# Row-wise first load and nearer stores in a bias-and-softmax kernel

## The chip, the core and the metric

The kernel runs on one core of a Trainium2 chip. The metric is the device time of one launch in microseconds; the time before is the median of ten runs.

## The reference

The kernel adds a clipped relative position bias to a batch of attention logits and takes a softmax over the last axis. There are 2 x 8 matrices of 2112 x 2112 floats; each of the 8 heads has 33 bias values.

```python
rel_clipped = np.clip(pos[:, None] - pos[None, :], -16, 16) + 16
logits = logits + rel_bias[:, rel_clipped][None]
logits = logits - logits.max(axis=-1, keepdims=True)
exp = np.exp(logits)
return (exp / exp.sum(axis=-1, keepdims=True)).astype(np.float32)
```

285.5 MB come in and 285.5 MB go out. (The kernel leaves out the subtraction of the maximum, which doesn't change the quotient.)

## The kernel before

The 33,792 rows are dealt out to the 128 partitions, 264 consecutive rows to each. A chunk is R = 4 rows of every partition: 128 x 8448 floats, 4224 KB, and there are N = 66 chunks. Five buffers L0 to L4 hold chunks; a chunk is loaded, changed in place and stored from the same buffer.

Four queues work on them, each with its order written out by hand, and they meet through semaphores:

- SP (`block.sync`) loads the first five chunks, one DMA each, then for each later chunk waits until the store from its buffer has landed (`reload`, L93) and loads again. Its DMAs are queue q1 of the profile.
- DVE (`block.vector`) first builds the strip F (`strip_of`, L140), 2343 floats on each partition, from which the bias of any row is a window. For that it waits for the bias table rbP (the wait ahead of L168). Then, for each chunk (`vec`, L122): wait until it is loaded, two adds of two rows each (L110), and, as soon as the sums of two rows are there, a reciprocal (L129) and two multiplies (L133).
- ACT (`block.scalar`) issues the two DMAs of the bias table (L205), then for each chunk takes the exponentials row by row with the sum beside it (`exps`, L112, L119). ACT also issues the stores (L91), on queue q10. A store is put into `exps` as `first`: it is issued once the first add of that chunk is done, which by DVE's order means that the chunk before has been multiplied to its end.
- POOL fills two small index tables at the start.

Before the change the store of chunk n - 2 is issued in the exponentials of chunk n ("two chunks behind"), from chunk 2 on; chunk 65, the last, issues stores 63 and 64, and store 65 follows when DVE has finished. The loops take five chunks a turn so that each body names a fixed buffer; what is left over is written out.

A wait takes the semaphore down again by what it waited for (`take`, L84), so that the same constants serve in every turn. L85 in the profile is that wait.

Of the kernel before, what the change touches and what calls it, by code (L numbers as in the profile page):

```python
# [14 lines left out]
def kernel(  # L15
# [14 lines left out]

    nc = tc.nc
    P = 128
    B, H, S, S2 = logits.shape
# [4 lines left out]
    T = S // Q  # L40
    assert Q * B * H == P and T * Q == S and T % W == 0
    M = T // W
    R = 4
    HALF = 2
    BUFS = 5
    N = T // R
# [2 lines left out]
    NB = (FW - 2 * MR) // W  # L49
    assert NB * W + 2 * MR == FW  # L50
    RS = R * S
    PASSES = (N - BUFS - 1) // BUFS
    REST = PASSES * BUFS

    const = ctx.enter_context(tc.tile_pool(name="const", bufs=1))
    F = const.tile([P, FW], FP32, tag="F", name="F")
# [8 lines left out]
    L = [const.tile([P, RS], FP32, tag=f"L{u}", name=f"L{u}") for u in range(BUFS)]  # L65
    tot = [const.tile([P, R], FP32, tag=f"tot{u}", name=f"tot{u}") for u in range(BUFS)]

    def rows(t, start):
        return bass.AP(
            tensor=t.tensor, offset=t.offset + start * S, ap=[[T * S, P], [1, RS]]  # L70
        )

    section = ctx.enter_context(tc.tile_critical(name="rows"))  # L73
    loaded = [nc.alloc_semaphore(f"loaded{u}") for u in range(BUFS)]
# [9 lines left out]
    def take(eng, sem, v):  # L84
        eng.wait_ge(sem, v).then_inc(sem, -v)  # L85

    def load(eng, u, start):
        eng.dma_start(out=L[u][:], in_=rows(logits, start)).then_inc(loaded[u], 16)

    def store(eng, u, start):  # L90
        eng.dma_start(out=rows(out, start), in_=L[u][:]).then_inc(stored[u], 16)  # L91

    def reload(eng, u, start):  # L93
        take(eng, stored[u], 16)
        load(eng, u, start)

    def add(eng, u, s0, start):
        x = L[u]
        x3 = bass.AP(
            tensor=x.tensor,  # L100
            offset=x.offset + (s0 + HALF - 1) * S,
            ap=[[list(x.ap[0])[0], P], [-S, HALF], [1, S]],
        )

        F3 = bass.AP(
            tensor=F.tensor,
            offset=(F.offset + T - HALF - s0) - start,
            ap=[[list(F.ap[0])[0], P], [1, HALF], [1, S]],
        )
        eng.tensor_tensor(out=x3, in0=x3, in1=F3, op=ALU.add).then_inc(added, 1)  # L110

    def exps(eng, u, first):  # L112
        for s0 in range(0, R, HALF):
            take(eng, added, 1)
            if s0 == 0:
                first()
            for i in range(s0, s0 + HALF):
                x = L[u][:, i * S : (i + 1) * S]
                e = eng.activation(out=x, in_=x, func=EXP, accum_out=tot[u][:, i : i + 1])  # L119
            e.then_inc(summed, 1)  # L120

    def vec(eng, u, start, last=False):  # L122
        take(eng, loaded[u], 16)
        for s0 in range(0, R, HALF):
            add(eng, u, s0, start)
        for s0 in range(0, R, HALF):
            take(eng, summed, 1)
            t = tot[u][:, s0 : s0 + HALF]
            eng.reciprocal(out=t, in_=t).then_inc(inverted, 1)  # L129
            take(eng, inverted, 1)  # L130
            for i in range(s0, s0 + HALF):
                x = L[u][:, i * S : (i + 1) * S]
                e = eng.tensor_scalar_mul(out=x, in0=x, scalar1=tot[u][:, i : i + 1])  # L133
        if last:
            e.then_inc(scaled, 1)

    def strip_of(eng):  # L140

        assert M * Q & (M * Q - 1) == 0
        low = rbP[:, W - 1 : W]
        high = rbP[:, 0:1]
        pitch = list(F.ap[0])[0]
        blocks = bass.AP(tensor=F.tensor, offset=F.offset + MR, ap=[[pitch, P], [W, NB], [1, W]])
        rev = bass.AP(
            tensor=rbP.tensor,
            offset=rbP.offset + W - 1,
            ap=[[list(rbP.ap[0])[0], P], [0, NB], [-1, W]],  # L150
        )

        def wide(t):
            return bass.AP(
                tensor=t.tensor, offset=t.offset, ap=[[list(t.ap[0])[0], P], [1, NB], [0, W]]
            )

        def step(ins):
            ins.then_inc(strip, 1)
            take(eng, strip, 1)  # L160

        take(eng, blocks_ready, 2)
        step(eng.tensor_single_scalar(out=qi[:], in_=qi[:], scalar=M * Q - 1, op=ALU.bitwise_and))  # L163
        step(eng.tensor_tensor(out=qm[:], in0=qi[:], in1=mm[:], op=ALU.subtract))  # L164
        for m, op in ((eq, ALU.is_equal), (lt, ALU.is_gt), (gt, ALU.is_lt)):
            step(eng.tensor_scalar(out=m[:], in0=qm[:], scalar1=0.0, scalar2=None, op0=op))  # L166
        take(eng, table, 16 * B)
        step(eng.tensor_scalar(out=rest[:], in0=lt[:], scalar1=low, scalar2=None, op0=ALU.mult))  # L168
        step(eng.tensor_copy(out=F[:, 0:MR], in_=low.to_broadcast([P, MR])))  # L169
        step(  # L170
            eng.scalar_tensor_tensor(  # L171
                out=rest[:], in0=gt[:], scalar=high, in1=rest[:], op0=ALU.mult, op1=ALU.add
            )
        )
        step(eng.tensor_copy(out=F[:, FW - MR : FW], in_=high.to_broadcast([P, MR])))  # L175
        step(eng.tensor_tensor(out=blocks, in0=wide(eq), in1=rev, op=ALU.mult))  # L176
        step(eng.tensor_tensor(out=blocks, in0=blocks, in1=wide(rest), op=ALU.add))  # L177

    with nc.Block() as block:  # L179

        @block.sync
        def _(eng):
            for u in range(BUFS):
                load(eng, u, u * R)
            with eng.Fori(BUFS * R, (REST + BUFS) * R, BUFS * R) as i:
                for u in range(BUFS):
                    reload(eng, u, i + u * R)
            for n in range(REST + BUFS, N):
                reload(eng, n % BUFS, n * R)
            for n in range(N - BUFS, N):  # L190
                take(eng, stored[n % BUFS], 16)

        @block.gpsimd
        def _(eng):
            eng.iota(qi[:], pattern=[[0, NB]], base=0, channel_multiplier=M).then_inc(  # L195
                blocks_ready, 1
            )
            eng.iota(mm[:], pattern=[[1, NB]], base=1 - M, channel_multiplier=0).then_inc(  # L198
                blocks_ready, 1
            )  # L200

        @block.scalar
        def _(eng):
            for b in range(B):
                eng.dma_start(  # L205
                    out=rbP[b * H * Q : (b + 1) * H * Q],
                    in_=bass.AP(
                        tensor=rel_bias.tensor,
                        offset=rel_bias.offset,
                        ap=[[W, H], [0, Q], [1, W]],  # L210
                    ),
                ).then_inc(table, 16)
            def none():
                pass

            def behind(u, start):
                return lambda: store(eng, (u - 2) % BUFS, start - 2 * R)

            for n in range(2):
                exps(eng, n, none)  # L220
            with eng.Fori(2 * R, (REST + 2) * R, BUFS * R) as i:
                for u in range(BUFS):
                    exps(eng, (u + 2) % BUFS, behind(u + 2, i + u * R))
            for n in range(REST + 2, N - 1):
                exps(eng, n % BUFS, behind(n, n * R))
            exps(
                eng,
                (N - 1) % BUFS,
                lambda: [store(eng, n % BUFS, n * R) for n in (N - 3, N - 2)],
            )  # L230
            take(eng, scaled, 1)
            store(eng, (N - 1) % BUFS, (N - 1) * R)

        @block.vector
        def _(eng):
            strip_of(eng)
            with eng.Fori(0, REST * R, BUFS * R) as i:
                for u in range(BUFS):
                    vec(eng, u, i + u * R)
            for n in range(REST, N):  # L240
                vec(eng, n % BUFS, n * R, last=n == N - 1)


# [28 lines left out]
```

## Time and profile before

| what | us |
|---|---|
| median of ten runs | 1353.92 (1351.43 to 1354.94) |
| the profiled execution's own time | 1355.21 |
| its span | 1353.4 |
| DVE busy | 960.6 |
| ACT busy | 527.0 |
| bytes moved | 571.00 MB, 422 GB/s over the span |

The span is the time that the profiler covers; what lies around it, 1.8 us, is start and end of the launch. Busy times of the engines overlap each other. The row "DMA" of the page divides the span into 40 slices of 33.8 us and gives the busy share of the 16 DMA engines in each, in tenths.

### The profile page before, as it was taken

The numbers are of one execution on the slowest core, as the hardware profiler recorded it, in microseconds if no ns is written. First come the engines' busy times: TensorE is split into PE (matmuls) and PEld (weight loads), VectorE is DVE, ScalarE is ACT, GpSimd is POOL, SyncE is SP. The second block draws the span as 40 slices with busy tenths as digits, with TensorE's granted clock in tenths as the row PEclk, the third lists the DMA queues.
The fourth block names the chain that finished last, engine by engine and source line by source line (L and its number), as shares of the span: only waits on it lengthen the run. The fifth ranks groups of instructions, "written<-read, shape, count | busy, mean of one in ns | idle before, by whom it ended". The sixth has DMA issues, their size and how long they took to land. (4 is left out here: it accounts for less than half of the span.)

```text
span 1353.4 us, 2458 instructions
## 1 busy us (share of the span) xinstructions
DVE 960.6 (71%) x539; ACT 527.0 (39%) x529; POOL 0.5 (0%) x6
## 2 busy tenths in 40 slices
DVE  1888776776776677677677677677667767767762
ACT  0544433442442443443343344244244334334432
POOL 0000000000000000000000000000000000000000
DMA  9579999999999999999999999999999999999988
GB/s 395 245 318 430 432 431 432 431 433 438 433 433 431 432 431 432 431 433 438 435 431 431 431 433 430 432 438 435 433 431 431 431 432 431 433 439 434 432 376 384
DMA packets 19155, 571.00 MB, mean 422 GB/s; under 512 B 2256, under 2 KB 2256, under 8 KB 2256
## 3 DMA queue, kind: packets, MB, share of 16 engines
q1 hardware_dynamic: 9504, 285.48, 49.1%
q10 hardware_dynamic: 9648, 285.50, 48.9%
q14 instruction: 3, 0.02, 0.0%
HBM read 285.49 MB, written 285.47 MB: 422 GB/s over the span
## 5 line engine op out<-in xcount | busy, mean ns | idle before, releaser
L119 ACT ACTIVATE L<-L 128x2112 f32<-128x2112 f32 x264 | 516.0, 1955 | 761.9 <-ACTq L85 761.6
L110 DVE TENSOR_TENSOR L<-L,F 128x4224 f32<-128x4224 f32 x132 | 595.7, 4554 | 230.3 <-DVEq L85 230.3
L133 DVE TENSOR_SCALAR L<-L,tot 128x2112 f32<-128x2112 f32 x264 | 336.3, 1316 | 20.1 <-DVEq L85 0.5
L129 DVE RECIPROCAL tot<-tot 128x2 f32<-128x2 f32 x132 | 21.9, 166 | 93.3 <-DVEq L85 93.3
L119 ACT ACTIVATION_READ_ACCUMULATOR L<-L 128x1 f32 x264 | 49.2, 186 | 0.0
L168 DVE TENSOR_SCALAR rest<-lt,rbP 128x71 f32<-128x71 f32 x1 | 0.3, 257 | 24.4 <-DVEq L85 24.4
L119 ACT ACT_TABLE_LOAD x1 | 1.3, 1283 | 39.6 <-ACTq L85 39.6
L176 DVE TENSOR_TENSOR F<-eq,rbP 128x2343 f32<-128x2343 f32 x1 | 2.6, 2600 | 0.1
L177 DVE TENSOR_TENSOR F<-F,rest 128x2343 f32<-128x2343 f32 x1 | 2.6, 2599 | 0.1
L163 DVE TENSOR_SCALAR qi<-qi 128x71 int32<-128x71 int32 x1 | 0.2, 198 | 1.5 <-DVEq L85 1.5
L171 DVE SCALAR_TENSOR_TENSOR rest<-gt,rbP,rest 128x71 f32<-128x71 f32 x1 | 0.3, 293 | 0.2 <-DVEq L85 0.2
L164 DVE TENSOR_TENSOR qm<-qi,mm 128x71 f32<-128x71 int32 x1 | 0.2, 233 | 0.1
L166 DVE TENSOR_SCALAR eq<-qm 128x71 f32<-128x71 f32 x1 | 0.2, 198 | 0.2 <-DVEq L85 0.2
L166 DVE TENSOR_SCALAR lt<-qm 128x71 f32<-128x71 f32 x1 | 0.2, 197 | 0.1
L166 DVE TENSOR_SCALAR gt<-qm 128x71 f32<-128x71 f32 x1 | 0.2, 197 | 0.1
L169 DVE COPY F<-rbP 128x16 f32<-128x16 f32 x1 | 0.2, 175 | 0.1
L175 DVE COPY F<-rbP 128x16 f32<-128x16 f32 x1 | 0.2, 175 | 0.1
L195 POOL IOTA qi<- 128x71 int32 x1 | 0.2, 187 | 0.6 <-SPq L73 0.6
L198 POOL IOTA mm<- 128x71 int32 x1 | 0.2, 187 | 0.0
L256 POOL MEMSET const-bfloat16-1.0<- 128x1 bf16 x1 | 0.1, 101 | 0.0
L256 POOL MEMSET const-uint8-127<- 128x1 uint8 x1 | 0.1, 101 | 0.0
L256 POOL MEMSET const-float32-0.0<- 128x1 f32 x1 | 0.1, 98 | 0.2 <-issue 0.2
(1 smaller groups left out, 0.1 us busy)
## 6 DMA issues: line engine op xcount, KB each, us to landing
L<-in_logits_dram SPq DMA_DIRECT2D x66, 4224.0 KB, 27.3
out_dram<-L ACTq DMA_DIRECT2D x66, 4224.0 KB, 27.4
rbP<-in_rel_bias_dram ACTq DMA_DIRECT2D x2, 8.2 KB
```

The costliest lines, as they stand in the source:

```text
L110: eng.tensor_tensor(out=x3, in0=x3, in1=F3, op=ALU.add).then_inc(added, 1)
L119: e = eng.activation(out=x, in_=x, func=EXP, accum_out=tot[u][:, i : i + 1])
L129: eng.reciprocal(out=t, in_=t).then_inc(inverted, 1)
L133: e = eng.tensor_scalar_mul(out=x, in0=x, scalar1=tot[u][:, i : i + 1])
L163: step(eng.tensor_single_scalar(out=qi[:], in_=qi[:], scalar=M * Q - 1, op=ALU.bitwise_and))
L164: step(eng.tensor_tensor(out=qm[:], in0=qi[:], in1=mm[:], op=ALU.subtract))
L166: step(eng.tensor_scalar(out=m[:], in0=qm[:], scalar1=0.0, scalar2=None, op0=op))
L168: step(eng.tensor_scalar(out=rest[:], in0=lt[:], scalar1=low, scalar2=None, op0=ALU.mult))
L171: eng.scalar_tensor_tensor(out=rest[:], in0=gt[:], scalar=high, in1=rest[:], op0=ALU.mult, op1=ALU.add)
L176: step(eng.tensor_tensor(out=blocks, in0=wide(eq), in1=rev, op=ALU.mult))
L177: step(eng.tensor_tensor(out=blocks, in0=blocks, in1=wide(rest), op=ALU.add))
L256: nc = _bacc.Bacc("TRN2", target_bir_lowering=False, num_devices=1)
```

## The change

- The first chunk is loaded with four DMAs, one for each row of a partition, on the same semaphore; DVE waits once until all four have landed and sets the counter back to what its ordinary wait expects.
- The exponentials of chunks 1 to 5 issue the store of the chunk before (one behind). Those of chunk 6 issue none. From chunk 7 on the store is two behind, as before. Chunk 64 issues stores 62 and 63, chunk 65 store 64, and store 65 follows at the end.
- The three loops are made by one helper, `passes`, which takes the range of chunks; the places where the loops start and end move a little.

```diff
-    def rows(t, start):
+    def rows(t, start, run=RS):
         return bass.AP(
-            tensor=t.tensor, offset=t.offset + start * S, ap=[[T * S, P], [1, RS]]
+            tensor=t.tensor, offset=t.offset + start * S, ap=[[T * S, P], [1, run]]
         )
...
+    def passes(eng, n0, n1, body):
+
+        k = (n1 - n0) // BUFS * BUFS
+        with eng.Fori(n0 * R, (n0 + k - BUFS) * R + 1, BUFS * R) as i:
+            for u in range(BUFS):
+                body((n0 + u) % BUFS, i + u * R)
+        for n in range(n0 + k, n1):
+            body(n % BUFS, n * R)
...
         @block.sync
         def _(eng):
-            for u in range(BUFS):
+            for r in range(R):
+                eng.dma_start(
+                    out=L[0][:, r * S : (r + 1) * S], in_=rows(logits, r, S)
+                ).then_inc(loaded[0], 16)
+            for u in range(1, BUFS):
                 load(eng, u, u * R)
-            with eng.Fori(BUFS * R, (REST + BUFS) * R, BUFS * R) as i:
-                for u in range(BUFS):
-                    reload(eng, u, i + u * R)
-            for n in range(REST + BUFS, N):
-                reload(eng, n % BUFS, n * R)
+            passes(eng, BUFS, N, lambda u, start: reload(eng, u, start))
...
         @block.scalar
...
-            for n in range(2):
-                exps(eng, n, none)
-            with eng.Fori(2 * R, (REST + 2) * R, BUFS * R) as i:
-                for u in range(BUFS):
-                    exps(eng, (u + 2) % BUFS, behind(u + 2, i + u * R))
-            for n in range(REST + 2, N - 1):
-                exps(eng, n % BUFS, behind(n, n * R))
-            exps(
+            def out_of(*ns):
+                return lambda: [store(eng, n % BUFS, n * R) for n in ns]
+
+            exps(eng, 0, out_of())
+            for n in range(1, NEAR - 1):
+                exps(eng, n % BUFS, out_of(n - 1))
+            exps(eng, (NEAR - 1) % BUFS, out_of())
+            passes(
                 eng,
-                (N - 1) % BUFS,
-                lambda: [store(eng, n % BUFS, n * R) for n in (N - 3, N - 2)],
-            )
+                NEAR,
+                N - 2,
+                lambda u, start: exps(
+                    eng, u, lambda: store(eng, (u - 2) % BUFS, start - 2 * R)
+                ),
+            )
+            exps(eng, (N - 2) % BUFS, out_of(N - 4, N - 3))
+            exps(eng, (N - 1) % BUFS, out_of(N - 2))
             take(eng, scaled, 1)
             store(eng, (N - 1) % BUFS, (N - 1) * R)
...
         @block.vector
         def _(eng):
             strip_of(eng)
-            with eng.Fori(0, REST * R, BUFS * R) as i:
-                for u in range(BUFS):
-                    vec(eng, u, i + u * R)
-            for n in range(REST, N):
-                vec(eng, n % BUFS, n * R, last=n == N - 1)
+            eng.wait_ge(loaded[0], 16 * R).then_inc(loaded[0], 16 - 16 * R)
+            passes(eng, 0, N - 1, lambda u, start: vec(eng, u, start))
+            vec(eng, (N - 1) % BUFS, (N - 1) * R, last=True)
```

NEAR is 7.

More of the change, by code (lines that the diff above doesn't have):

```diff
@@ L51 @@
     RS = R * S
-    PASSES = (N - BUFS - 1) // BUFS
-    REST = PASSES * BUFS
+    NEAR = 7
     const = ctx.enter_context(tc.tile_pool(name="const", bufs=1))
@@ L212, in _ @@
                 ).then_inc(table, 16)
[L213 to L217, printed above, removed]
-            for n in range(2):
-                exps(eng, n, none)
-            with eng.Fori(2 * R, (REST + 2) * R, BUFS * R) as i:
-                for u in range(BUFS):
-                    exps(eng, (u + 2) % BUFS, behind(u + 2, i + u * R))
-            for n in range(REST + 2, N - 1):
-                exps(eng, n % BUFS, behind(n, n * R))
-            exps(
-                eng,
-                (N - 1) % BUFS,
-                lambda: [store(eng, n % BUFS, n * R) for n in (N - 3, N - 2)],
-            )
+            def out_of(*ns):
[5 more added lines that the diff above has]
+            passes(
+                eng,
+                NEAR,
[3 more added lines that the diff above has]
+                ),
+            )
+            exps(eng, (N - 2) % BUFS, out_of(N - 4, N - 3))
+            exps(eng, (N - 1) % BUFS, out_of(N - 2))
             take(eng, scaled, 1)
```

## The prediction

> **What bounds the kernel now.** I read the page's first three parts, then the chain, then the busy time by stretches of the span, then the timeline at both ends.
>
> ```profile
> span 1353.4 us, 2458 instructions
> DVE 960.6 (71%) x539; ACT 527.0 (39%) x529; POOL 0.5 (0%) x6
> DMA  9579999999999999999999999999999999999988
> q1 hardware_dynamic: 9504, 285.48, 49.1%
> q10 hardware_dynamic: 9648, 285.50, 48.9%
> HBM read 285.49 MB, written 285.47 MB: 422 GB/s over the span
> ```
>
> No engine is full; the 16 DMA engines are, except in slices 2, 3 and the last two. The load queue (q1) and the store queue (q10) carry the same bytes. The chain of waits is only 2.6 us long (a DVE multiply and a queue step at 1329 to 1331.5): it loses the trail at the stores, so I leave it aside and go by stretches. Columns: stretch, its length, busy time of three engines, clock, DMA share, GB/s.
>
> ```profile
> 0.00:14.00 14.00, 1.02 (x5) 0.00 (x0) 0.52 (x6) 1.00 0.86 348
> 14.00:25.00 11.00, 0.00 (x0) 0.00 (x0) 0.00 (x0) 1.00 1.02 428
> 25.00:35.00 10.00, 6.17 (x7) 0.00 (x0) 0.00 (x0) 1.00 1.01 433
> 35.00:55.00 20.00, 17.58 (x9) 9.18 (x9) 0.00 (x0) 1.00 0.90 387
> 55.00:74.40 19.40, 17.60 (x10) 9.37 (x9) 0.00 (x0) 1.00 0.07 28
> 74.40:95.00 20.60, 18.41 (x12) 12.48 (x15) 0.00 (x0) 1.00 0.93 367
> 95.00:125.00 30.00, 27.06 (x14) 13.79 (x14) 0.00 (x0) 1.00 1.00 424
> ...
> 155.00:1290.00 1135.00, 821.28 (x456) 454.16 (x456) 0.00 (x0) 1.00 1.00 433
> ...
> 1315.00:1332.00 17.00, 14.45 (x8) 7.89 (x8) 0.00 (x0) 1.00 0.75 319
> 1332.00:1353.40 21.40, 0.00 (x0) 0.00 (x0) 0.00 (x0) 1.00 0.84 363
> ```
>
> With loads alone (25 to 35) and with both queues (155 to 1290) the rate is 433 GB/s at share 1.00. 571.00 MB at 433 is 1318.7 us; the other 34.7 us of the span are DMA time not used. By stretch it is length x (1 - rate/433): the start 2.7; 14 to 35 0.1; 35 to 125 2.1 + 18.1 + 3.1 + 0.6 = 24.0; the last two 4.5 and 3.5. These add up to 34.9. So the time is set by the moments in which neither queue has work, and by nothing else. The timeline says why they are empty:
>
> ```profile
> 27.51 0.26 DVE L168 TENSOR_SCALAR rest<-lt,rbP 128x71 f32<-128x71 f32 x1 [24.37 <-DVEq L85]
> 31.75 2.60 DVE L177 TENSOR_TENSOR F<-F,rest 128x2343 f32<-128x2343 f32 x1
> 34.93 9.03 DVE L110 TENSOR_TENSOR L<-L,F 128x4224 f32<-128x4224 f32 x2 [0.58 <-DVEq L85]
> 56.39 1.96 ACT L119 ACTIVATE L<-L 128x2112 f32<-128x2112 f32 x1 [7.60 <-ACTq L85]
> 72.61 0.38 ACTq L91 DMA_DIRECT2D out_dram<-L  x1
> 1319.74 0.82 ACTq L91 DMA_DIRECT2D out_dram<-L  x2
> 1331.62 0.34 ACTq L91 DMA_DIRECT2D out_dram<-L  x1
> ```
>
> DVE waits 24.37 us for the 16 KB bias table; the strip F is done at 34.35, and chunk 0's add starts at 34.93. All five buffers are loaded by about 55; the first store is issued at 72.61, with the exponentials of chunk 2. Between, nothing can move. At the end, stores 63 and 64 are issued at 1319.74, while by the packet records store 62 ends at 1316.4 and the next packets start at 1321.6: a hole of 5.2 us, most of the 4.5 of that stretch.
>
> **The change, part by part.**
> *Row loads beside the bias table.* Chunk 0 comes as four DMAs of 1056 KB, 8,448 bytes a partition, instead of one of 33,792. The packet records show that the bias DMAs use 8 of the 16 engines, 18 small packets on each, and that from 7.3 us on each of these waits for one whole load packet of 1.251 us: 18 x 1.25 = 22, so 27.5 at DVE is explained. A quarter-size packet is 1.251/4 = 0.31 us; with the small packet and the gaps 0.33. 18 x 0.33 = 6, so the table lands near 13.4 us, if its first packet still comes at 7.3. From that point L168 to chunk 0's add is 34.93 - 27.51 = 7.4 us: add at 20.8. Chunk 0 itself has landed by then (14.0 before).
> [...] The packet records show turns of one descriptor: one bias packet every 1.25 us beside 33,792-byte ones. [...]
> Cost of the split: SP issues 8 DMAs instead of 5, at 0.333 us each (the median of the load issues), so its last first-round load leaves at 4.6 instead of 3.6 us; load 1 isn't needed in the queue before 14, and load 5's reload is queued behind them but waits for store 0 anyway. [...] I take 0.7, between 0 and 6.
> DVE's added wait on the four rows (then the counter set back) is one more step in its queue, some 0.1 us (steps of the strip follow each other at 0.1 to 0.2); behind it is only chunk 0's add, which it can't delay beyond the landing.
>
> *Stores one chunk behind at first.* Store 0 moves from the exponentials of chunk 2 to those of chunk 1: 56.39 - 34.93 = 21.5 us after chunk 0's add, so at 20.8 + 21.5 = 42.3 instead of 72.61. Its packets follow 1.8 us later (72.61 to 74.4 before): 44.1, while loads 3 and 4 still run (to 55 alone, to about 65 with the store beside them). So store 0 ends at about 64, load 5 is queued at 66, while store 1 (issued 16 us after store 0, at 58.4) moves. From there one queue always has work: DVE's period of 16.07 us (51.72 to 67.79) is shorter than DMA's 20.0 for a load and a store. So all of the 24.0 goes. ACT's issue of 0.34 us ahead of chunk 1 costs nothing: DVE's period was 16.07 without a store (chunk 1) and with one (chunk 2). If it were uncovered, 5 x 0.34 = 1.7. What is late next: DVE, which in chunks 1 to 7 comes after its loads; DMA doesn't wait for it.
>
> *The switch at chunk 6.* No store is issued there; store 5 goes with chunk 7. Chunk 7's add is at 20.8 + 16.8 + 6 x 16.07 = 134, store 5 in the queue at 141. Store 4 ends, with stores at 20 us each after store 0's 64, at about 144. So the queue has some 3 us left; and if it ran dry, load packets would have the engines to themselves. Cost 0, at most some 5. The middle is as before, two behind: 0 per chunk.
>
> *The last four.* Chunk 64's exponentials issue stores 62 and 63, so 63 is there when 62 ends: -4.5 (the stretch) to -5.2 (the hole). Two issues take 0.82 instead of 0.34 us on ACT, ahead of chunk 64's exponentials; DVE is idle 3.85 us ahead of each late add, which hides it. Store 64 goes at chunk 65's add as before, store 65 after the last multiply, 16.5 us after that add; store 63 and 64 are 20 us of cover. The last stretch's 3.5 us (landing of the last store) stay.
>
> *Loops.* DVE's loop makes 13 turns instead of 12, ACT's body starts elsewhere, register steps of 0.03 to 0.05 us: under DMA, 0.
>
> Sum: -24.0 - 4.5 + 0.7, and 0.5 for seams that remain: -27.3. On the profiled execution's span 1353.4 this gives 1326.1, on its own time 1355.2 it gives 1327.9. The median of the runs is 1.3 below that execution, 1353.9: I predict 1326.6. A floor: 1318.7 + 2.7 + 3.5 = 1324.9 of span.
>
> **The rivals.**
> [...] Chance 0.11.
> *A hole at the switch or at the end*, some 5 us, because the phase between the queues differs: 1331. For it: the slack of about 3 us. Against: both queues must be dry at once. Chance 0.08.
> *Slower: a lower rate in the middle.* Loads and stores then meet at other places of HBM, store boundaries about 3 us from where they were against the loads. If reads and writes disturbed each other there, each per cent of 433 GB/s in the 1135 us would cost 11.4; at 2.4%, below 423 GB/s, all the gain is gone, and at 3% the time is 1361. For it: nothing in the trace excludes it. Against: the rate is the same 433 with loads alone as with both, at share 1.00, so the engines are the limit, not where the data lie. Chance 0.04. That the change does nothing, both holes staying, can't be: store 0's issue doesn't need chunk 2. I leave 0.02 for it and the like.
>
> **How the numbers follow.** The main case, 0.75, lies between the floor, 1324.9 + 0.5, and 1329 (most of the 6 us rule for the DMAs excluded by the rows). The range goes from 1324.5 to 1335, with the second case and most of the first. About 0.2% (2.7 us) is what a measurement of this kernel tells from no change. Faster 0.94, within 0.02, slower 0.04.
>
> **What would show it.** Right: L168 at 13 to 14 us and the first add near 21; first store issued near 42; share 1.00 between 35 and 125; no stretch under 400 GB/s between 1270 and the last landing; 433 in the middle. Wrong in the first step: L168 later than 24, the add later than 32, an empty stretch after 55. Wrong in the switch: a dip at 135 to 160. Wrong in the whole: a middle below 430 GB/s.

## The result and the profile after

The changed kernel takes 1331.34 us (median of nine runs, 1329.72 to 1340.27) against 1354.06 before (30 runs, 1351.43 to 1355.11): ratio 0.9847, 95% interval 0.9834 to 0.9859, so 22.7 us less by the medians. The profiled execution took 1327.64 us, with a span of 1325.9; it is the shortest of the eleven executions on record here. Both numbers matter: the sum of the prediction met the span of that one execution (1326.1 against 1325.9), but the median lies 4.7 us above the predicted 1326.6, inside the range. The page after:

```profile
span 1325.9 us, 2476 instructions
DVE 960.4 (72%) x539; ACT 527.1 (40%) x529; POOL 0.5 (0%) x6
DMA  9999999999999999999999999999999999999998
q1 hardware_dynamic: 9936, 285.48, 50.0%
q10 hardware_dynamic: 9648, 285.50, 49.9%
HBM read 285.49 MB, written 285.47 MB: 431 GB/s over the span
```

The two slices that showed 5 and 7 tenths are full, and the engines' busy times are as they were. q1 has 432 packets more: 3 x 128 data packets of 8,448 bytes, and 3 x 16 of 4 bytes, 16 at the end of each DMA. The same stretches as before the change (stretch, length, busy time of DVE, ACT, POOL, clock, DMA share, GB/s):

```profile
0.00:14.00 14.00, 3.13 (x10) 0.00 (x0) 0.53 (x6) 1.00 0.88 340
...
35.00:55.00 20.00, 17.89 (x10) 8.01 (x8) 0.00 (x0) 1.00 0.98 411
55.00:74.40 19.40, 17.70 (x10) 9.20 (x9) 0.00 (x0) 1.00 1.03 442
74.40:95.00 20.60, 18.57 (x12) 12.44 (x13) 0.00 (x0) 1.00 0.98 422
...
125.00:155.00 30.00, 24.31 (x16) 12.12 (x14) 0.00 (x0) 1.00 1.00 433
155.00:1240.00 1085.00, 787.13 (x437) 435.99 (x437) 0.00 (x0) 1.00 1.00 433
...
1305.00:1325.90 20.90, 0.00 (x0) 0.00 (x0) 0.00 (x0) 1.00 0.80 346
```

The stretch from 55 to 74.4 went from 28 to 442 GB/s. By length x (1 - rate/433), 35 to 95 now loses 1.0 - 0.4 + 0.5 = 1.1 us, where it lost 23.3. The middle stays at 433, and nothing dips at 125 to 155, where the stores go from one chunk behind to two. The timeline at both ends:

```profile
11.29 0.26 DVE L178 TENSOR_SCALAR rest<-lt,rbP 128x71 f32<-128x71 f32 x1 [8.16 <-DVEq L86]
18.83 9.03 DVE L111 TENSOR_TENSOR L<-L,F 128x4224 f32<-128x4224 f32 x2 [0.70 <-DVEq L86]
40.28 0.36 ACTq L92 DMA_DIRECT2D out_dram<-L  x1
...
1273.64 0.94 ACTq L92 DMA_DIRECT2D out_dram<-L  x2
1293.35 0.34 ACTq L92 DMA_DIRECT2D out_dram<-L  x1
1304.96 0.34 ACTq L92 DMA_DIRECT2D out_dram<-L  x1
```

The table is used at 11.29 instead of 27.51, chunk 0's add starts 16.1 us earlier, the first store 32.3 us earlier. The last store goes out at 1304.96, 21 us before the end: nearly two stores of 10 us each (4224 KB at 433 GB/s) are then left to drain.

### The profile page after: what moved, and what is told of

Its sections match the earlier page's. It is cut to its first block, busy times and chain, and to the rows that moved or that the text cites. A ratio compares the mean times of both kernels' runs of the same rounds, so it can differ in the third digit from the quotient of the medians.

```text
span 1325.9 us, 2476 instructions
## 1 busy us (share of the span) xinstructions
DVE 960.4 (72%) x539; ACT 527.1 (40%) x529; POOL 0.5 (0%) x6
## 6 DMA issues: line engine op xcount, KB each, us to landing
out_dram<-L ACTq DMA_DIRECT2D x66, 4224.0 KB, 27.5
```

## The experiments

Each run was timed in rounds beside the kernel before; the three batches had 1353.23, 1353.06 and 1353.32 us for it. Unless said otherwise, the edit is against the changed kernel.

**The changed kernel again**, unedited, in two batches.

> The changed kernel once more, unedited, to see how far its executions lie apart. Its profiled execution had a span of 1325.9 us, 0.2 from the sum, but the median of its runs was 1331.3 and two were at 1338 and 1340. Theory (bytes at 433 GB/s plus the moments without work): 1326 to 1328 of span in every execution, and the later ones are chance. Rival 1 (thin slack of the two-behind middle, about 3 us in each queue, runs dry in some executions): a spread of some 10 us again, while the kernel with one-behind stores throughout shows none. Rival 2 (the start differs between executions): the spread goes with the row loads.

> The changed kernel once more, for the spread (3 of 15 executions so far lay at 1338 to 1340). Thin-slack theory: one or more of five at 1335 to 1340. Median 1330 to 1333 by both.

Medians 1332.62 (1327.53 to 1338.58) and 1330.12 (1327.24 to 1338.62). Of all 22 executions, four lie at 1338 to 1340, the others at 1327 to 1334. The first expectation's theory, a span of 1326 to 1328 in every execution, has fallen. This time the profiled execution was a long one, with a span of 1336.8:

```profile
155.00:900.00 745.00, 538.45 (x298) 296.50 (x297) 0.00 (x0) 1.00 1.00 433
900.00:1300.00 400.00, 282.15 (x159) 157.57 (x160) 0.00 (x0) 1.00 1.00 428
1300.00:1336.80 36.80, 14.46 (x8) 8.01 (x8) 0.00 (x0) 1.00 0.74 318
```

The first profile of the same kernel over the same first two stretches, and its end:

```profile
155.00:900.00 745.00, 540.75 (x300) 299.99 (x301) 0.00 (x0) 1.00 1.00 433
900.00:1300.00 400.00, 290.11 (x162) 160.25 (x163) 0.00 (x0) 1.00 1.00 433
1300.00:1325.90 25.90, 3.46 (x4) 1.84 (x2) 0.00 (x0) 1.00 0.84 363
```

Until 900 us both run at 433. Then the long one falls to 428 (400 x 5/433 = 4.6 us) and its end leaves 36.8 x (1 - 318/433) = 9.8 us unused against 4.2: 10.2 of the 10.9 us between them. The packet records (each packet's start, duration, size and queue) say more. Each load or store ends with 16 packets of 4 bytes, by their times one on each DMA engine. In the short execution the 16 of one load lie 2.7 us apart all through the middle. In the long one they spread from 2.5 us at the start to 7 us by 900 and 13 us at the end: one DMA engine falls behind, while each chunk waits for all 16. And packets take longer: from 900 to 1300 us, 147 of 5072 full packets took 1.3 to 2.5 us instead of 1.25, most of them from 940 us on; in the short execution it was one of 5129. All that the packets of that stretch took beyond 1.25 us is 77 us, or 4.8 us for each of the 16 engines: the 4.6 us lost there. The DMA share stays at 1.00, so the queues did not run dry in the middle.

**Stores one behind throughout**, in two batches.

```diff
-            exps(eng, (NEAR - 1) % BUFS, out_of())
+            exps(eng, (NEAR - 1) % BUFS, out_of(NEAR - 2))
...
-                    eng, u, lambda: store(eng, (u - 2) % BUFS, start - 2 * R)
+                    eng, u, lambda: store(eng, (u - 1) % BUFS, start - R)
...
-            exps(eng, (N - 2) % BUFS, out_of(N - 4, N - 3))
+            exps(eng, (N - 2) % BUFS, out_of(N - 3))
```

> Stores one chunk behind throughout: the exponentials of chunk 6 issue store 5, the loop's body stores the chunk before, chunk 64 issues store 63, chunk 65 store 64. Theory: the middle is bound by the 16 DMA engines at 433 GB/s, so the distance of the stores is worth nothing there: 1326 of span, within 1 us of the changed kernel. Rival 1 (thin slack): median 3 to 5 us below the changed kernel and a spread of under 4 us. Rival 3 (a queue full of stores disturbs the loads): slower by 5 us or more.

> Stores one behind throughout once more, for the spread. Thin-slack theory: again nothing above 1333. Chance: one or two of five at 1335 or more.

1331.59 (1329.90 to 1332.42), then 1331.22, but with one execution at 1343.90. The stores do wait longer: here, and in the changed kernel, the issues of the stretch 900 to 1250 with their median time from issue to landing, last column:

```profile
L<-in_logits_dram SPq DMA_DIRECT2D x18, 4224.0 KB, 27.3
out_dram<-L ACTq DMA_DIRECT2D x17, 4224.0 KB, 47.4
```

```profile
L<-in_logits_dram SPq DMA_DIRECT2D x18, 4224.0 KB, 27.0
out_dram<-L ACTq DMA_DIRECT2D x17, 4224.0 KB, 27.5
```

A store issued 20 us earlier lands no earlier; it only waits longer in its queue. The distance of the stores in the middle is worth nothing measurable, as predicted. After the first batch I took the thin slack of the two-behind middle for the cause of the long executions; the one at 1343.90 in a kernel with 20 us more slack speaks against that as the whole cause.

**The first load whole, stores as changed.**

```diff
-            for r in range(R):
-                eng.dma_start(
-                    out=L[0][:, r * S : (r + 1) * S], in_=rows(logits, r, S)
-                ).then_inc(loaded[0], 16)
+            load(eng, 0, 0)
...
-            eng.wait_ge(loaded[0], 16 * R).then_inc(loaded[0], 16 - 16 * R)
```

> Chunk 0 again as one DMA of 4224 KB, stores as in the changed kernel. Theory: the bias table lands at 27.5 and the first add starts at 34.9 as before the change, store 0 is issued at 56.4, DMA is empty for 3 + 1.6 + 2 us: span 1332.5, 20.9 below the kernel before. Rival (the row loads are the whole gain, the stores none): 1347 or more. Rival 2 (the spread comes from the row loads): this kernel has none.

1338.47 (1336.66 to 1351.26), 14.8 us below before. The first store goes at 56.65, as expected, but the head loses more than the 3 + 1.6 + 2 = 6.6 us:

```profile
35.00:55.00 20.00, 17.38 (x9) 9.18 (x9) 0.00 (x0) 1.00 0.89 384
55.00:74.40 19.40, 17.70 (x10) 9.29 (x9) 0.00 (x0) 1.00 0.81 333
74.40:95.00 20.60, 18.57 (x12) 12.45 (x13) 0.00 (x0) 1.00 0.97 395
```

2.3 + 4.5 + 1.8 = 8.6 us unused. Of the head's 24.0 this leaves a gain of 15.4, near the 14.8 measured. The other 4.5 us of the expectation, the hole at the end, are not there. It also has two long executions of six, with no row loads, so rival 2 falls.

**Row loads, stores two behind throughout.**

```diff
-            for n in range(1, NEAR - 1):
-                exps(eng, n % BUFS, out_of(n - 1))
-            exps(eng, (NEAR - 1) % BUFS, out_of())
+            exps(eng, 1, out_of())
             passes(
                 eng,
-                NEAR,
+                2,
...
-            exps(eng, (N - 2) % BUFS, out_of(N - 4, N - 3))
-            exps(eng, (N - 1) % BUFS, out_of(N - 2))
+            exps(eng, (N - 2) % BUFS, out_of(N - 4))
+            exps(eng, (N - 1) % BUFS, out_of(N - 3, N - 2))
```

> Row loads of chunk 0, stores two behind throughout as before the change (65 issues 63 and 64). Theory: first add near 18.8, first store 16 us earlier than before the change, at about 56.5; of the 24.0 us of the head some 14 to 16 go and the hole of 5 us at the end stays: span 1338 to 1340. Rival (stores are the whole gain): 1353.

1336.09 (1334.95 to 1338.22, four runs), 17.1 us below before. The three stretches from 35 to 95, and the one with the hole at the end:

```profile
35.00:55.00 20.00, 17.79 (x10) 8.00 (x8) 0.00 (x0) 1.00 0.90 387
55.00:74.40 19.40, 17.69 (x10) 9.10 (x9) 0.00 (x0) 1.00 0.81 334
74.40:95.00 20.60, 18.44 (x12) 12.50 (x13) 0.00 (x0) 1.00 1.00 411
...
1290.00:1305.00 15.00, 11.34 (x4) 3.54 (x3) 0.00 (x0) 1.00 0.86 372
```

2.1 + 4.4 + 1.0 = 7.5 us are unused in the head, which makes 16.5 of gain. The profiled span, 1333.5, is below the expected 1338 to 1340, which counted the hole at the end with 5 us: its place here still runs at 372 GB/s, and the gain of the head alone is nearly all of the 17.1. So each half of the change alone brings 15 to 17 us and both 21 to 23: they work on one hole, and add to much less than 32.

**The end alone, on the kernel before.** Against the kernel before, in its last chunks (the loops made by the helper as in the changed kernel; the lines with a minus are the old end, written that way):

```diff
-            exps(eng, (N - 2) % BUFS, out_of(N - 4))
-            exps(eng, (N - 1) % BUFS, out_of(N - 3, N - 2))
+            exps(eng, (N - 2) % BUFS, out_of(N - 4, N - 3))
+            exps(eng, (N - 1) % BUFS, out_of(N - 2))
```

> The kernel before with one edit: chunk 64 issues stores 62 and 63, chunk 65 store 64 (one load for chunk 0, two behind from chunk 2). Theory A, as the prediction had it: the hole of 5.2 us between stores 62 and 63 goes, 1349 instead of 1353.4. Theory B (the 16 DMA engines drift apart, the last of them 6.6 us behind the median at the end of the profiled execution before; the hole is where the others wait and the late one catches up): the late engine has next to no hole, so 1352 to 1354, and the 16 completions of the last store lie 4 to 7 us apart instead of 0.9.

1352.21 (1350.91 to 1354.61, 11 runs) against 1353.06: ratio 0.9995, interval 0.9986 to 1.0004. The profiled execution, the shortest of the eleven, has no hole at the end:

```profile
1315.00:1332.00 17.00, 9.83 (x7) 8.00 (x8) 0.00 (x0) 1.00 0.99 425
1332.00:1349.10 17.10, 0.00 (x0) 0.00 (x0) 0.00 (x0) 1.00 0.75 322
```

The stretch of 17 us went from 319 to 425 GB/s, and the median moved by 0.9 us, within the error. The spread of the last store's 16 end packets says why. Before, the engines are 6.7 us apart at store 61; the hole brings them to 1.0 us at store 63, and they end 0.9 us apart. Without the hole they keep what they have: 2.4 us at store 62 and 2.5 at the end of this execution, less than the 4 to 7 that theory B expected.

**The changed kernel with the old end.**

```diff
-            exps(eng, (N - 2) % BUFS, out_of(N - 4, N - 3))
-            exps(eng, (N - 1) % BUFS, out_of(N - 2))
+            exps(eng, (N - 2) % BUFS, out_of(N - 4))
+            exps(eng, (N - 1) % BUFS, out_of(N - 3, N - 2))
```

> The changed kernel with the end as before the change: chunk 64 issues store 62, chunk 65 stores 63 and 64. Theory A: 5 us slower than the changed kernel, 1331 at best and 1336 in the median. Theory B: the same median as the changed kernel, 1331 to 1333, with the completions of the last store within 1 us.

1330.70 (1328.93 to 1333.99), the same as with the new end, and 0.6 us between the last end packets. Theory B's times hold on both kernels: at the end the early DMA engines waited, the late one did not.

**Stores of the middle 4.4 us later.**

```diff
-    def exps(eng, u, first):
+    def exps(eng, u, first, at=0):
...
-            if s0 == 0:
+            if s0 == at:
...
-                    eng, u, lambda: store(eng, (u - 2) % BUFS, start - 2 * R)
+                    eng, u, lambda: store(eng, (u - 2) % BUFS, start - 2 * R), at=HALF
```

> The changed kernel with the loop's stores (chunks 7 to 61) issued 4.4 us later in the same chunk, after two of its four exponentials. DMA-bound theory: slack of about 6 us in the two queues together is left at 1 to 2, nothing lost, 1331 as the changed kernel. Thin-slack theory (an engine that drifts by some us eats the slack, one queue runs dry on the others, and each restart costs): below 430 GB/s through the middle in most executions, 1340 or more in the median.

1330.52 in the median (1329.00 to 1340.11), so the 6 us of slack could be cut to 1 or 2 at no cost in five of six executions. The profiled one was the long one, 1338.3 of span:

```profile
900.00:1300.00 400.00, 280.88 (x159) 158.21 (x160) 0.00 (x0) 1.00 1.00 425
```

Here too the packets account for it: what they took beyond 1.25 us is 7.5 us for each engine in that stretch, and 400 x (1 - 425/433) = 7.4.

**Chunk 0 in two DMAs.**

```diff
-            for r in range(R):
+            for r in range(0, R, 2):
                 eng.dma_start(
-                    out=L[0][:, r * S : (r + 1) * S], in_=rows(logits, r, S)
+                    out=L[0][:, r * S : (r + 2) * S], in_=rows(logits, r, 2 * S)
                 ).then_inc(loaded[0], 16)
...
-            eng.wait_ge(loaded[0], 16 * R).then_inc(loaded[0], 16 - 16 * R)
+            eng.wait_ge(loaded[0], 16 * 2).then_inc(loaded[0], 16 - 16 * 2)
```

> Chunk 0 in two DMAs of 2112 KB instead of four of 1056, all else as changed. If a bias packet waits for one load packet (now 16,896 bytes, 0.63 us): table at DVE near 16 to 18 us, between 11.3 with four and 27.5 with one, first add at 24 to 26, time as the changed kernel since the add is still before 32. [...]

```profile
20.27 0.26 DVE L178 TENSOR_SCALAR rest<-lt,rbP 128x71 f32<-128x71 f32 x1 [17.14 <-DVEq L86]
27.80 9.03 DVE L111 TENSOR_TENSOR L<-L,F 128x4224 f32<-128x4224 f32 x2 [0.69 <-DVEq L86]
49.26 0.36 ACTq L92 DMA_DIRECT2D out_dram<-L  x1
65.73 0.34 ACTq L92 DMA_DIRECT2D out_dram<-L  x1
66.09 20.47 SPq L89 DMA_DIRECT2D L<-in_logits_dram  x2
```

One, two and four DMAs put the table at 27.5, 20.3 and 11.3 us. With one and two, the packet records show every bias packet behind one load packet, whatever its size; the table is later than the 16 to 18 us expected because from 13 us on the packets beside it are those of load 1, of full size. With four it is otherwise (see the account of the table below). The time is 1335.72 (1333.56 to 1345.53, four runs), 3 to 6 us above the changed kernel's medians, though the add, at 27.8, is before the 32 us that I had taken as the limit. Three stretches of this profile:

```profile
55.00:64.00 9.00, 7.24 (x6) 2.74 (x4) 0.00 (x0) 1.00 0.89 384
64.00:66.00 2.00, 2.00 (x2) 0.00 (x0) 0.00 (x0) 1.00 0.04 17
66.00:74.40 8.40, 6.84 (x5) 8.00 (x8) 0.00 (x0) 1.00 1.01 382
```

The five loads and store 0 have drained by 64 on most engines and by 65.8 on the last, and both the reload and store 1 are issued only near 66: 1.0 + 1.9 + 1.0 = 3.9 us lost.

**The bias table ahead of the loads**, in SP's own queue, chunk 0 whole; then the same with stores one behind throughout.

```diff
         @block.sync
-            for r in range(R):
+            for b in range(B):
                 eng.dma_start(
-                    out=L[0][:, r * S : (r + 1) * S], in_=rows(logits, r, S)
-                ).then_inc(loaded[0], 16)
+                    out=rbP[b * H * Q : (b + 1) * H * Q],
...
+                ).then_inc(table, 16)
+            load(eng, 0, 0)
...
         @block.scalar
         def _(eng):
-            for b in range(B):
-                eng.dma_start(
-                    out=rbP[b * H * Q : (b + 1) * H * Q],
...
         @block.vector
         def _(eng):
             strip_of(eng)
-            eng.wait_ge(loaded[0], 16 * R).then_inc(loaded[0], 16 - 16 * R)
```

> The two bias DMAs are issued by SP ahead of the loads, in the loads' own queue; chunk 0 in one DMA of 4224 KB, DVE's extra wait gone, stores as in the changed kernel. In-order theory: 16 bias packets and their two ends pass ahead of the first load packet, the table is at DVE by 5 to 7 us, chunk 0 lands at about 15 and its add starts near 16 (18.8 in the changed kernel); time within 1 us of the changed kernel, since any add before 26 us is covered. Rival (the split itself spares something, chunk 0's packets being smaller): 3 us or more slower.

> Bias DMAs ahead of the loads on SP as in the run before, and stores one behind throughout. If thin slack makes the long executions: 1329 to 1332 in every one, no execution of 1335 or more. If they are chance in any kernel whose DMA is never empty: one in five or six at 1335 or more here too.

With stores as changed:

```profile
3.89 0.26 DVE L178 TENSOR_SCALAR rest<-lt,rbP 128x71 f32<-128x71 f32 x1 [0.76 <-DVEq L86]
15.46 9.03 DVE L111 TENSOR_TENSOR L<-L,F 128x4224 f32<-128x4224 f32 x2 [4.73 <-DVEq L86]
```

The table is used at 3.89, the add starts at 15.46 (3.94 and 15.36 with stores one behind). Times: 1330.40 (1330.07 to 1331.38) and 1330.44 (1330.26 to 1330.60). So the row loads are worth what they do for the table's arrival, and nothing beyond. Neither version beats the changed kernel, 1330.12 on the same chip, by its median; their spread is 1.3 and 0.3 us instead of 11.

## Why the prediction was right, and where not

*The bound.* Right: DMA at 433 GB/s and moments without work. That the losses of all stretches add up to the span less 1318.7 us is arithmetic; what shows it is that they lay where the queues were empty, and that filling these cut the loss from 35 to 95 us from 23.3 to 1.1. "By nothing else" is too much: the two long executions profiled lose 5 to 7 us in the middle to packets that take longer.

*The table and the first add.* The table came at 11.3 and the add at 18.8, instead of 13.4 and 20.8: 2 us off, and the mechanism is only half right. The prediction's times of packets run 0.9 us ahead of the timeline's clock (on that clock the first bias packet before came at 6.4, not 7.3; 17 more turns of 1.25 us then give 27.6, where 7.3 + 22 gives 29), and the first bias packet now comes 3.0 us after the first load packet instead of 4.4. From the first to the last bias packet it takes 5.9 us, where 6 were forecast, but not as 18 turns. Where the load of the first row ends, the nine packets of the first bias DMA pass in one run on most of its eight engines, with no load packet between them: all 72 start between 4.99 and 6.03 us, where nine turns beside load packets of 0.32 us would take 2.9. Only those of the second pass between load packets, until 10.84. That the sum of 6 us came out is luck. In the kernel before and with two DMAs all 18 go one behind each load packet. Why the first nine pass in a run here is open. A chance of 0.11 was given to a table that stays late, with the add at 34.93 or after; the add came at 18.83.

*The cost of the split.* The sum takes 0.7 us, between 0 and 6. Both were my estimates: no run shows a loss of 0.7 us, and none shows the 6 us for the DMAs. What the runs showed in their place: before, the stretches 14 to 25 and 25 to 35, each with a boundary between two DMAs, lose 0.1 and 0 us; with three DMAs more, the start, 0 to 14, loses 3.0 us instead of 2.7, and 14 to 35 nothing.

*The head.* Right: 24.0 us were to go, and of them 1.1 are left. Store 0's packets came 3.7 us after its issue, at 43.97, not 1.8: beside running loads it took longer than before the change on idle engines, where it was 0.9 (72.61 to 73.49 on the timeline's clock). The loads covered that. But the limit for the add, 32 us (the end of the loads at 55.4, less 21.5 and 1.8), was wrong. I asked only that store 0 arrive while loads run. What has to hold is that work lasts until store 1 or the reload behind store 0 arrives. Six chunks of work from 2.0 us on end at about 64; store 1's packets come 21.5 + 16.1 + 0.9 = 38.5 us after the add. By this estimate the limit is near 25, and two DMAs, with 27.8, miss it.

*The switch, the middle, the loops.* Right: nothing lost at 125 to 155, 433 after it.

*The end.* This is the term that was mis-sized: 4.5 us in the sum, 0.9 us measured on the kernel before (interval -0.5 to +1.9 from the ratio) and nothing on the changed one. I read the hole from the mean over 16 engines, and the end of store 62 from the early ones. On the timeline's clock, 13 engines end store 62 by 1315.6, but the last at 1320.70, and it begins store 63 at 1320.71. Fourteen engines wait 4.4 to 5.5 us there, one waits 2.1, and the late one, which sets when the last store is complete, not at all. With the end at nothing to 0.9 us the sum gives 22.8 to 23.7 us, and 22.7 were measured. That the profiled span agreed with the full sum is luck: in that execution the engines ended 2.3 us apart. In a more usual one, with stores one behind throughout, they ended 5.7 apart, and the stretch from 1305 to the end left 6.9 us unused instead of 4.2:

```profile
900.00:1305.00 405.00, 292.75 (x164) 164.06 (x165) 0.00 (x0) 1.00 1.00 433
1305.00:1329.80 24.80, 2.71 (x3) 0.47 (x2) 0.00 (x0) 1.00 0.72 312
```

*What stays open.* Why an engine falls behind in some executions and not in others, and what makes the executions of 1338 us and more. The two profiles of such have in common that packets take longer late in the middle, which falls to 425 and 428 GB/s; in the one at 428 the engines drift to 13 us. What makes those packets longer is not shown. Executions as long as that came with and without row loads, and with thin and with ample slack. None is among the ten with the table ahead of the loads, where no engine carries table packets between load packets; ten are too few to call that a cause. Before the change there is none either: its holes may be the reason, since at the one near the end the engines came together again (6.7 us to 1.0). This was not tried for the hole at 55 to 74; without the one near the end, eleven runs had no long execution either.

## What to carry to other kernels

When DMA is the bound, add up the stretches in which it has no work and ask for each what would have to be issued earlier; two edits on one hole didn't add here (14.8 and 17.1 us alone, 22.7 together). Before counting a hole at the end, look at it engine by engine: where the engines have drifted apart, a hole in the mean is where the early ones wait, and filling it moves the last one little (here 0.9 us for a hole of 4.5). A small table needed first goes ahead of the large loads in their own queue (3.89 us here), or beside small packets (11.29 us, beside 8,448 bytes); both did the same for the time here, 1330.40 and 1330.12.

## What the runs showed of the hardware that was not expected

- The 16 DMA engines of one core drifted apart, by up to 7 us in an ordinary execution and 13 us in a long one, although each has 8 packets of every chunk. A moment without work brought them together (6.7 us to 1.0 us at the end of the kernel before).
- Beside a full load queue, a bias packet of the other queue passed after each load packet, of 33,792 or 16,896 bytes alike: the 16 KB table came at 27.5 and 20.3 us. Beside packets of 8,448 bytes it came at 11.3, with nine packets in a run on most engines where one load DMA ended; ahead of the loads, at 3.9.
- With both queues full, a store issued 20 us earlier landed at the same time: 47.4 us from issue to landing instead of 27.5.
- In the executions of 1338 us and more that were profiled, packets took longer than 1.25 us (up to 2.5 us in the first; from 900 to 1300 us, 4.8 and 7.5 us more for each engine) at a DMA share of 1.00, and the rate fell from 433 to 428 and 425 GB/s: a full DMA row on the page did not show that the rate held.
